# Hi/lo splits of the first dense expert blocks, moved from VectorE to GpSimd

## The chip, the cores and the metric

The kernel runs on one core of a Trainium2 chip. The metric is the device time of one execution in microseconds (us), the median of several runs. The core has a tensor engine (PE in the profile, with its weight loads as PEld), VectorE (DVE), ScalarE (ACT), GpSimd (POOL) and SyncE (SP, which here only issues DMAs). GpSimd also issues the gathers of table rows, as indirect DMAs. Each engine works through its own queue in order.

## The reference

One layer of a decoder, for 1024 prompt positions and 8 x 4 sample positions together (1056 tokens of 1024 features, float32): an RWKV-7 mixer and a pooling mixer with their projections, then a PEER feed-forward, then a gated per-layer embedding and a last norm. The change concerns PEER, cut here to what matters:

```python
q = (xb @ wq).reshape(PEER_BLOCK, PEER_HEADS, 2, PEER_DK_HALF)
s1 = jnp.einsum('thc,nc->thn', q[:, :, 0], sub_keys[0])
s2 = jnp.einsum('thc,nc->thn', q[:, :, 1], sub_keys[1])
v1, i1 = lax.top_k(s1, PEER_TOPK)
v2, i2 = lax.top_k(s2, PEER_TOPK)
...
sc, ci = lax.top_k(cand, PEER_TOPK)
...
expert = e1 * N_KEYS + e2
gate = jax.nn.softmax(sc.astype(jnp.float32), axis=-1)
ue = jnp.take(u_tab, expert, axis=0)
act = jax.nn.gelu(jnp.einsum('thkd,td->thk', ue, xb), approximate=False) * gate
ve = jnp.take(v_tab, expert, axis=0)
return jnp.einsum('thk,thkd->td', act, ve)
```

For each token and each of 8 heads, 16 of 16384 experts are chosen by two top-16 lists over 128 keys each and a top-16 over their sums. Each chosen expert is one row of a table u (a dot product with the token, then gelu times the gate) and one row of a table v (added with that weight).

## The kernel before

The kernel is one program in which a scheduler sets each engine's order: instructions are given in program order, and it places them by that order as priority and by when it takes their inputs to be ready. The order of each queue is fixed when the program is built.

**Stages.** Up to about 1380 us of the profile come the projections, the two mixers, the output projection, and for all tokens the queries and key scores of PEER. Then two ways of computing PEER run side by side:

- Tokens 0 to 671 (GA to GB, ND = 672 columns) are done densely, over all 16384 experts. The experts lie in 128 blocks of 128 (EB = 128). The gates of a token, zero for the experts that it hasn't chosen, were built before and lie in HBM (g_d).
- Tokens 672 to 1055 (384 columns in three tiles of 128) are done by rows: each chosen row of u and v is gathered, and VectorE multiplies and adds (lines 1193 to 1233). For a tile that is 256 gathers. They are issued on GpSimd (line 1202), into 7 row buffers (NROW). The u rows meet line 1210 on VectorE, the v rows lines 1217 and 1219.

**The float32 products in three parts.** A float32 product is made as three products of a faster form: both factors are split into a high part (a rounded copy, made on ScalarE) and a low part (the difference, made with one subtraction), and high x high, high x low and low x high are added up in PSUM. The low parts are what the change moves. Function `esplit` (lines 1065 to 1072) loads a weight block of 128 x 1024 (eraw, 3 buffers, a 512 KB DMA on SP), makes ehi on ScalarE (line 1069, 2 buffers) and elo with the operation that it is given (line 1071, 2 buffers). Function `emm` (lines 1087 to 1093) issues the 48 products of one weight block: 8 blocks of the contracted dimension, three parts each, two halves of 336 columns.

**The dense loop.** For expert block b:

- `ublock(b)` (line 1095) splits the u weights, multiplies them with the tokens (XH, XL) and puts gelu of the result into U[b] (line 1099). For blocks 0 to 7 this was done earlier, by `upre` (line 1101), whose splits are already on GpSimd: `PTT` (line 123) is GpSimd's tensor_tensor, and the profile shows all its instructions under line 124. `TT` is VectorE's.
- `ugate(b)` (line 1144) multiplies with the gates (line 1150, VectorE), copies to the high part wh (line 1152, ScalarE) and subtracts to the low part wl (line 1154). wh and wl have 9 buffers each, in the pool dw, which is opened (line 1140) when the pools of the query stage have been closed (cstack, line 1139). The last users of those pools are the products with the keys on line 747.
- After each eight blocks (VG = 8) `vblock(g, db)` runs for the 8 output blocks db: it splits a block of the v weights, multiplies it with the eight wh and wl, and puts the sum into OT[db] (line 1164 for the first group, line 1162, an addition on VectorE, for the later ones). One group with its 8 output blocks is called a sum, or a round, here.

`dense(0, NB0)` with NB0 = 18 runs blocks 0 to 17 and the sums of groups 0 and 1. It stands in the program between `gtop(0)` and the other two calls of `gtop` (lines 1134 to 1138 and 1182). `gtop` makes the top-16 lists for one tile of the row part (function `top`, line 753): long sequences of max, index search and replacement on VectorE, with some small products on GpSimd (codes, line 793 by way of line 124; one-hot times gate, line 848, whose sum is taken on VectorE, line 850). Only after the third `gtop` are the pools closed whose memory the row buffers take (line 1184), so the gathers start after it. `dense(NB0, EB + 1)` (line 1191) runs the rest of the dense part, and the row part stands behind it in the program and fills in.

At the end come the gated embedding and the last norm, for the dense tokens (`td`) and the tokens of the row part (`tg`).

Of the kernel before, what the change touches and what calls it, by code (L numbers as in the profile page):

```python
# [10 lines left out]
F32 = mybir.dt.float32  # L11
# [5 lines left out]
ALU = mybir.AluOpType  # L17
# [34 lines left out]
VG = 8  # L52
# [9 lines left out]
def body(ctx, tc, io):  # L62
    nc = tc.nc
    mm = nc.tensor.matmul
    TT, STT, TS, ACT = (nc.vector.tensor_tensor, nc.vector.scalar_tensor_tensor, nc.vector.tensor_scalar,
                        nc.scalar.activation)
# [995 lines left out]
    def PD():  # L1062
        return dps.tile([128, 2, 512], F32, name="pd")

    def esplit(src, sub=TT):
        raw = dr.tile([128, KB, 128], F32, name="eraw", bufs=3)
        nc.sync.dma_start(raw, src)
        hi = dr.tile([128, KB, 128], F32R, name="ehi", bufs=2)
        ACT(hi, raw, AF.Copy)  # L1069
        lo = dr.tile([128, KB, 128], F32R, name="elo", bufs=2)  # L1070
        sub(lo, raw, hi.bitcast(F32), op=ALU.subtract)  # L1071
        return hi, lo
# [3 lines left out]
    def otile(db):  # L1076
        if db not in OT:
            OT[db] = (dr if db < KB - 1 else late).tile([128, ND], F32, name=f"OT{db}")
        return OT[db]

    def wt_tile():
        return late.tile([128, ND], F32, name="wt", bufs=NWT)

    def halves(t):
        return t.rearrange("p (a b) -> p a b", a=2)

    def emm(ps, w, xs, parts):
        wh_, wl_ = w
        for k in range(KB):
            xh, xl = xs[k]  # L1090
            for w_, x_, first, last in ((wh_, xh, k == 0, False), (wh_, xl, False, False), (wl_, xh, False, k == KB - 1)):
                for a, (s, n) in enumerate(parts):
                    mm(ps[:, a, :n], w_[:, k, :], x_[:, s:s + n], start=first, stop=last)  # L1093

    def ublock(b, sub=TT):
        ps = PD()
        emm(ps, esplit(io["uT"][b], sub), xs, DP)
        U[b] = otile(b) if b < NPRE else wt_tile()
        ACT(halves(U[b]), ps[:, :, :NH], AF.Gelu)
# [41 lines left out]

    Ws, gqs = {}, {}

    def ugate(b):
        if b % GQ == 0:
            gqs[0] = gqp.tile([128, NTC, GQ, TC], F32, name="gq")
            nc.sync.dma_start(gqs[0], g_d[b // GQ])
        wt_ = U[b]
        w3 = wt_.rearrange("p (c t) -> p c t", t=TC)
        TT(w3, w3, gqs[0][:, :, b % GQ, :], op=ALU.mult)  # L1150
        wh = dw.tile([128, ND], F32R, name="wh", bufs=VG + 1)
        ACT(wh, wt_, AF.Copy)
        wl = dw.tile([128, ND], F32R, name="wl", bufs=VG + 1)
        TT(wl, wt_, wh.bitcast(F32), op=ALU.subtract)
        Ws[b] = (wh, wl)

    def vblock(g, db):
        w = esplit(io["vP"][g, db])
        ps = PD()
        emm(ps, w, [Ws[b] for b in range(g * VG, (g + 1) * VG)], DP)  # L1160
        if g:
            TT(halves(OT[db]), ps[:, :, :NH], halves(OT[db]), op=ALU.add)  # L1162
        else:
            ACT(halves(OT[db]), ps[:, :, :NH], AF.Copy)
        if g == EB // VG // 2:
            ht = wt_tile()
            nc.sync.dma_start(ht, hT_d[:, db, GA:GB])
            TT(OT[db], OT[db], ht, op=ALU.add)

    def dense(b0, b1):  # L1170
        for b in range(b0, b1):
            if b < EB:
                if b not in U:
                    ublock(b)
                ugate(b)
            if b % VG == 0 and b:
                for db in range(KB):
                    vblock(b // VG - 1, db)

    NB0 = 2 * VG + 2  # L1180
    dense(0, NB0)
    for col in range(128, GT, 128):
        gtop(col)
    phases.close()
# [4 lines left out]
    dpt = ctx.enter_context(tc.tile_pool(name="dpt", bufs=2, space=bass.MemoryType.PSUM, reuse_waits="tile"))  # L1189

    dense(NB0, EB + 1)

    for col in range(0, GT, 128):
# [185 lines left out]
def program(arrays, extra=()):  # L1379
    nc = bacc.Bacc("TRN2", target_bir_lowering=False, num_devices=1)  # L1380
    io = {k: nc.dram_tensor(k, v.shape, mybir.dt.from_np(v.dtype), kind="ExternalInput").ap()
          for k, v in arrays.items()}
    for k, s in list(OUTS.items()) + list(extra):
        io[k] = nc.dram_tensor(k, s, F32, kind="ExternalOutput").ap()
    with tile.TileContext(nc, schedule_with_timeline_sim=True) as tc, ExitStack() as ctx:
        body(ctx, tc, io)
    return nc
# [15 lines left out]
```

## Time and profile before

| | us |
|---|---|
| median of 3 runs | 3357.13 |
| lowest and highest run | 3352.67, 3357.15 |
| the profiled execution | 3346.63 |
| its span, first to last instruction | 3344.9 |

| engine, in the profiled execution | busy us | share |
|---|---|---|
| PE | 3163.4 | 95% |
| PEld | 3063.6 | 92% |
| VectorE | 2661.9 | 80% |
| ScalarE | 1187.9 | 36% |
| GpSimd | 1803.7 | 54% |

The profile comes from one execution. It shows busy time by engine, by slices of the span and by groups of like instructions (line, engine, operation, output and inputs by the program's names, count, busy time and mean, then the idle time of the engine ahead of them and what ended it). In views of one tile or line, the three numbers after the count are the shortest, median and longest duration in ns, then the first and last start. A view in order of time has the start, the duration, the engine, the line and the operation; several like instructions in a row are one entry with xN. The chain of waits is followed back from the last instruction: at each step to what released it. The granted clock of the tensor engine is given as a share of its full speed; its mean over the span is 0.980. Matmuls are pipelined, and their ends are modelled.

### The profile page before, as it was taken

What the parts mean: (1) busy time and instruction counts of PE and PEld (TensorE: products, weight loads), DVE (VectorE), ACT (ScalarE), POOL (GpSimd) and SP (SyncE); (2) the same over time, 40 slices, a digit from 0 to 9 for tenths busy, and PEclk for the clock granted to TensorE, in tenths of its full rate; (3) what the DMA queues carried; (4) which work ended last, traced back from release to release, by engine and by line L of the source; (5) the groups of instructions that cost most, each with busy time, mean ns of one, the idle gap of its engine ahead of it and who ended that gap; (6) DMA issues with size and microseconds to landing.
All of it is one profiled execution on the core that took longest, in us unless ns stands there. A gap on an engine that the chain in (4) does not pass through costs nothing.

```text
span 3344.9 us, 57622 instructions
## 1 busy us (share of the span) xinstructions
PE 3163.4 (95%) x21831; PEld 3063.6 (92%) x21831; DVE 2661.9 (80%) x5365; ACT 1187.9 (36%) x1778; POOL 1803.7 (54%) x1434
## 2 busy tenths in 40 slices
PE   8997999998888888999999999999999999999997
PEld 7886989988878777899999999999999999999997
DVE  6777332359999989889888888888889888888966
ACT  6452523345555555431222222122122222222243
POOL 5434333235565456337666666666566666666635
PEclk9998999999999989999999999999999999999998
DMA  5568645667677787639999999999999999999933
GB/s 176 204 218 199 170 134 144 196 193 228 199 198 232 207 290 222 233 128 366 341 339 328 344 349 331 329 340 334 336 337 350 325 335 339 342 328 341 324 110 128
DMA packets 467861, 883.61 MB, mean 264 GB/s; under 512 B 129280, under 2 KB 252416, under 8 KB 463104
## 3 DMA queue, kind: packets, MB, share of 16 engines
q1 hardware_dynamic: 356992, 477.24, 44.3%
q0 software_dynamic: 110592, 402.70, 32.8%
q8 instruction: 171, 2.80, 0.3%
q14 instruction: 106, 0.87, 0.1%
HBM read 759.22 MB, written 120.60 MB: 263 GB/s over the span
## 4 chain that ended last, share of the span: by engine, by line
PE 69%; DVE 16%; DMA 4%; POOL 2%; issue 2%; ACT 1%; SPq 0%; DVEq 0%; ACTq 0%; POOLq 0%
PE pd L1093 57%; DVE ab L882 3%; DVE ab L883 2%; PE ps L663 1%; PE ps L661 1%; PE ps L662 1%; PE ps L526 1%; DMA sraw<-wq 1%; PE ps L521 1%; DVE oh L847 1%; DVE h L718 1%; DVE I L763 1%; DVE s L765 1%; DVE ab L884 1%; DVE I L767 1%
## 5 line engine op out<-in xcount | busy, mean ns | idle before, releaser
L1202 POOL DMA_INDIRECT row<-v,idx x384 | 543.4, 1415 | 314.2 <-DVE po L1219 142.6
L1202 POOL DMA_INDIRECT row<-u,idx x384 | 536.4, 1397 | 284.9 <-DVE row L1210 112.3
L1069 ACT ACTIVATE ehi<-eraw 128x1024 fp32r<-128x1024 f32 x278 | 295.0, 1061 | 1098.3 <-PE pd L1093 955.2
L1093 PE MATMUL pd<-XH,elo 128*128 128x336 f32 x2176 | 516.2, 318 | 6.1 <-DVE elo L1071 3.2
L1093 PE MATMUL pd<-XL,ehi 128*128 128x336 f32 x2176 | 515.4, 318 | 0.0
L1093 PE MATMUL pd<-XH,ehi 128*128 128x336 f32 x2176 | 512.5, 316 | 0.0
L1093 PE MATMUL pd<-wh,ehi 128*128 128x336 f32 (+1 forms) x2112 | 503.0, 317 | 6.2 <-DVE tg L1283 6.2
L1093 PE MATMUL pd<-wl,ehi 128*128 128x336 f32 (+1 forms) x2112 | 503.1, 317 | 0.0
L1093 PE MATMUL pd<-wh,elo 128*128 128x336 f32 (+1 forms) x2112 | 503.0, 317 | 0.0
L1219 DVE SCALAR_TENSOR_TENSOR po<-row,act,po 128x1024 f32<-128x1024 f32 x381 | 488.5, 1282 | 6.5
L1210 DVE SCALAR_TENSOR_TENSOR row<-row,xt 128x1024 f32<-128x1024 f32 x384 | 455.2, 1220 | 5.9 <-DMA row<-u,idx 5.8
L1071 DVE TENSOR_TENSOR elo<-eraw,ehi 128x1024 fp32r<-128x1024 f32 x256 | 318.3, 1243 | 79.8 <-ACT ehi L1069 67.8
L1093 PEld LDWEIGHTS pd<-XH,elo 128*128 128x128 f32 x2176 | 373.8, 189 | 7.8 <-DVE elo L1071 4.3
L1093 PEld LDWEIGHTS pd<-XH,ehi 128*128 128x128 f32 x2176 | 373.0, 189 | 0.3
L1093 PEld LDWEIGHTS pd<-XL,ehi 128*128 128x128 f32 x2176 | 371.2, 189 | 0.2
L1093 PEld LDWEIGHTS pd<-wh,ehi 128*128 128x128 f32 x2112 | 361.5, 188 | 6.9 <-issue 6.7
L1093 PEld LDWEIGHTS pd<-wh,elo 128*128 128x128 f32 x2112 | 362.0, 188 | 0.2
L1093 PEld LDWEIGHTS pd<-wl,ehi 128*128 128x128 f32 x2112 | 361.8, 188 | 0.0
L124 POOL TENSOR_TENSOR ab<-ab,e 128x512 f16<-128x512 f16 x110 | 132.0, 1202 | 160.8 <-DVE ab L883 127.5
L1162 DVE TENSOR_TENSOR OT<-pd,OT 128x672 f32<-128x672 f32 x120 | 102.9, 857 | 139.6 <-PE pd L1093 138.0
L889 ACT ACTIVATE gst<-ps 128x512 f32<-128x512 f32 x168 | 177.1, 1093 | 74.0 <-PE ps L887 72.8
L661 PE MATMUL ps<-hi,whi 128*128 128x256 f32 (+1 forms) x592 | 180.0, 305 | 12.0 <-DMA whi<-wc_d 7.4
(504 smaller groups left out, 5849.7 us busy)
## 6 DMA issues: line engine op xcount, KB each, us to landing
eraw<-uT SPq DMA_DIRECT2D x128, 512.0 KB
eraw<-vP SPq DMA_DIRECT2D x128, 512.0 KB
g_d<-gst SPq DMA_DIRECT2D x21, 2048.0 KB
gq<-g_d SPq DMA_DIRECT2D x32, 1344.0 KB
whi<-wc_d SPq DMA_DIRECT2D x148, 256.0 KB
wlo<-wc_d SPq DMA_DIRECT2D x148, 256.0 KB
wc_d<-shi SPq DMA_DIRECT2D x40, 256.0 KB
wc_d<-slo SPq DMA_DIRECT2D x40, 256.0 KB
```

What stands on the lines that cost most here:

```text
L124: nc.gpsimd.tensor_tensor(out, a, b, op=op)
L661: mm(ps[:, :n], whi[:, kk, :], xhi[:, k, :n], start=k == 0, stop=False)
L882: TT(ab[:, 0:4], iota16[:, None, :, :].to_broadcast([128, 4, EB, 2]), pairs(0, 4), op=ALU.is_equal)
L883: TT(ab[:, 4:6], ab[:, 2:4], pairs(2, 2), op=ALU.mult)
L889: ACT(st[:, :, t2:t2 + 4].rearrange("p e t -> p t e"), v3(ps, 128), AF.Copy, scale=1.0 / GS)
L1069: ACT(hi, raw, AF.Copy)
L1071: sub(lo, raw, hi.bitcast(F32), op=ALU.subtract)
L1093: mm(ps[:, a, :n], w_[:, k, :], x_[:, s:s + n], start=first, stop=last)
L1162: TT(halves(OT[db]), ps[:, :, :NH], halves(OT[db]), op=ALU.add)
L1202: nc.gpsimd.indirect_dma_start(out=r[:m], out_offset=None, in_=io[tab], in_offset=bass.IndirectOffsetOnAxis(ap=idx[:m, hh, k:k + 1], axis=0))
L1210: STT(r[:m], r[:m], 1.0, xt[:m], op0=ALU.mult, op1=ALU.mult, accum_out=pre[:m, k:k + 1])
L1219: STT(po[:m], r[:m], act[:m, k:k + 1], po[:m], op0=ALU.mult, op1=ALU.add)
```

## The change

The functions `ugate`, `vblock` and `dense` take a parameter `sub`, the operation that makes the low parts, and hand it on to `ublock` and `esplit`. Its default is VectorE's `TT`. The first call, `dense(0, NB0)`, now passes `PTT`, GpSimd's. In that call these instructions move from VectorE to GpSimd: elo of the u weights of blocks 8 to 17 (blocks 0 to 7 were made on GpSimd before, in `upre`), elo of the v weights of the sums of groups 0 and 1 (16 blocks), and wl of blocks 0 to 17. Each computes the same difference. The gate product (line 1150), the copies on ScalarE, the additions to OT and all DMAs stay on their engines, and the second call of `dense` is as before.

```diff
-    def ugate(b):
+    def ugate(b, sub=TT):
...
         wl = dw.tile([128, ND], F32R, name="wl", bufs=VG + 1)
-        TT(wl, wt_, wh.bitcast(F32), op=ALU.subtract)
+        sub(wl, wt_, wh.bitcast(F32), op=ALU.subtract)
         Ws[b] = (wh, wl)
 
-    def vblock(g, db):
-        w = esplit(io["vP"][g, db])
+    def vblock(g, db, sub=TT):
+        w = esplit(io["vP"][g, db], sub)
...
-    def dense(b0, b1):
+    def dense(b0, b1, sub=TT):
         for b in range(b0, b1):
             if b < EB:
                 if b not in U:
-                    ublock(b)
-                ugate(b)
+                    ublock(b, sub)
+                ugate(b, sub)
             if b % VG == 0 and b:
                 for db in range(KB):
-                    vblock(b // VG - 1, db)
+                    vblock(b // VG - 1, db, sub)
 
     NB0 = 2 * VG + 2
-    dense(0, NB0)
+    dense(0, NB0, PTT)
     for col in range(128, GT, 128):
         gtop(col)
```

## The prediction

> **What bounds the kernel now.** I read the page first, for where the tensor engine is full.
>
> ```profile
> span 3344.9 us, 57622 instructions
> PE   8997999998888888999999999999999999999997
> PEclk9998999999999989999999999999999999999998
> ```
>
> A slice is 83.6 us. From the seventeenth on (1338 us) PE is at nine tenths or more, to the last slice. The change touches work that starts at about 1386 us, so I then read the chain of work that ended last, in order of time, from there.
>
> ```profile
> 1388.41 3.67 PE pd L1093 x22
> ...
> 1393.19 114.30 PE pd L1093 x742
> 1507.49 1.21 DVE row L1210 x3
> 1508.70 1.15 DVE elo L1071
> 1509.90 543.09 PE pd L1093 x3525
> ...
> 3189.20 41.26 PE pd L1093 x267
> ...
> 3239.28 48.78 PE pd L1093 x312
> ```
>
> The chain is the dense products on line 1093 without a break, but for one piece of VectorE at 1507.5 us. I cut the stretch into slices of 10 us to see how much PE time is lost there at all.
>
> ```profile
> 1380.00:1390.00 10.00, 8.61 (x67) 8.12 (x66) 8.98 (x24) 5.42 (x7) 2.68 (x1) 1.00 1.00 399
> 1500.00:1510.00 10.00, 7.94 (x53) 7.66 (x51) 8.84 (x14) 2.33 (x3) 8.17 (x7) 1.00 1.00 400
> 1510.00:1520.00 10.00, 10.00 (x55) 10.00 (x56) 10.00 (x15) 4.43 (x6) 8.48 (x6) 0.83 0.95 364
> 1520.00:1530.00 10.00, 10.00 (x67) 10.00 (x66) 8.50 (x14) 1.96 (x3) 8.17 (x7) 1.00 0.99 388
> ```
>
> The columns are PE, PEld, DVE, ACT and POOL busy, then the granted clock and the DMA share. A full slice holds 67 products (0.15 us each). The two slices at 1500 us hold 53 and 55, so 26 are missing: 4.0 us, of which 2.06 is PE idle and 1.9 is the clock at 0.83 behind it. At 1380 us 1.4 us are idle and the clock stays at 1.00. So the stretch that the change works on has about 5 us to give back, whatever VectorE is relieved of. The relief itself is off the chain.
>
> **The splits and their prices.** In blocks 0 to 17 and in sums 0 and 1 the low halves go from VectorE to GpSimd: 10 of the u weights (blocks 0 to 7 are there already), 16 of the v weights, 18 of wl. No DMA is moved and SP's queue is unchanged. GpSimd's price for both shapes stands in the trace.
>
> ```profile
> L124 POOL TENSOR_TENSOR elo<-eraw,ehi x22: 2349/2410/3056, 1200.5 to 3320.0; 128x1024 fp32r<-128x1024 f32 x22
> ```
>
> ```profile
> L124 POOL TENSOR_TENSOR wl<-wl,tt x6: 1642/1647/2514, 3247.8 to 3283.4; 128x672 f32<-128x672 f32 x6
> ```
>
> A weight split costs 2.41 us and a wl of 672 columns 1.65 us (this row is another operation on the same shape; the weight row scaled by 672/1024 gives 1.58). GpSimd takes on 26 x 2.41 + 18 x 1.65 = 92.4 us. What stands behind a split on its queue is the top-k's small products (their gl reductions on VectorE wait) and the gathers.
>
> **Step 1, the burst at the first sum.** All eight wl of the first sum are made at once.
>
> ```profile
> 1391.91 1.28 PE L747 MATMUL ps<-keys,q 128*128 128x128 f32 x10
> ...
> 1396.42 0.47 PE L1093 MATMUL pd<-wh,ehi 128*128 128x336 f32 x2
> 1396.73 0.47 PE L1093 MATMUL pd<-wl,ehi 128*128 128x336 f32 x2
> ...
> 1397.34 0.47 PE L1093 MATMUL pd<-wh,ehi 128*128 128x336 f32 x2
> ```
>
> ```profile
> 1393.72 5.34 ACT L1152 ACTIVATE wh<-OT 128x672 fp32r<-128x672 f32 x8
> ```
>
> ```profile
> 1394.51 6.24 DVE L1154 TENSOR_TENSOR wl<-OT,wh 128x672 fp32r<-128x672 f32 x8 [1.10 <-ACT wh L1152]
> ```
>
> The wh cannot start before 1393.2: their buffers (dw) open only when the phase that ends with line 747 is closed. PE begins the sum at 1396.42 and goes one step (0.92 us) per block, so it wants wl number k at 1396.73 + 0.92 k, the last at 1403.2. VectorE makes one in 0.78 us and stays ahead. GpSimd, from 1394.5 at 1.65 us each, ends the last at 1407.7: PE stalls 4.5 us. Then wl of block 8, which stands ahead in program order, ends at 1409.4 and the next weight split at 1411.8, where PE wants it at 1408.9: 2.9 us more. A stall of that size is followed by a lower clock in the row at 1510 us, 1.9 us. Sum 9.3 us; with the block-8 wl behind the weight split and no clock loss it is 4.5 + 1.2 = 5.7. No slack covers this: PE has no other product that is ready. I take 9.3, as the order written in the program gives it. The split of u block 8, which VectorE does late at 1387.2, comes 0.5 us sooner: -0.5.
>
> By "TensorE: Matmul & The Clock Gate" of the Trainium skill (Part 1, What's actually happening) the clock falls to half only after an idle window of about 3.4 us. The trace's drop follows 2.06 us of idle, so by the page step 1 would cost 1.9 us less, and the measurement decides.
>
> **Step 2, the stall at 1507.5 goes.** There the weight split stands on VectorE behind row products that wait for their rows. On GpSimd it doesn't: -4.0 us.
>
> **Step 3, the splits beside the gathers.** The top-k is bound by VectorE, and the gathers start when it ends.
>
> ```profile
> 1492.72 0.41 DVE L850 TENSOR_REDUCE gl<-oh 128x16 f32<-128x256 f32 x1
> ...
> 1493.42 1.50 POOL L1202 DMA_INDIRECT row<-u,idx  x1 [1.71 <-DVE gl L850]
> ```
>
> ```profile
> L1071 DVE TENSOR_TENSOR elo<-eraw,ehi 128x1024 fp32r<-128x1024 f32 x15 | 20.6, 1370 | 0.2 <-ACT ehi L1069 0.2
> ...
> L1154 DVE TENSOR_TENSOR wl<-OT,wh 128x672 fp32r<-128x672 f32 x8 | 6.2, 853 | 1.1 <-ACT wh L1152 1.1
> ...
> L1154 DVE TENSOR_TENSOR wl<-wt,wh 128x672 fp32r<-128x672 f32 x4 | 4.0, 989 | 0.2 <-ACT wh L1152 0.2
> ```
>
> These are VectorE's splits between 1386 and 1493 us: 30.8 us, so the top-k ends up to 31 us sooner, at about 1465, and the gathers with it. The sums and blocks do not move, since PE sets them. One block or one sum is a slot of 7.35 us, the distance between two weight conversions on ACT:
>
> ```profile
> 1447.84 1.06 ACT L1069 ACTIVATE ehi<-eraw 128x1024 fp32r<-128x1024 f32 x1 [5.68 <-PE pd L1093]
> ...
> 1455.19 1.06 ACT L1069 ACTIVATE ehi<-eraw 128x1024 fp32r<-128x1024 f32 x1 [5.68 <-PE pd L1093]
> ```
>
> From 1396.4 on come 8 slots of the first sum, 8 blocks (9 to 16), 8 slots of the second sum and block 17. At 1465 the first sum and about two blocks are over; about 7 blocks and 8 sum slots are left, and in them GpSimd now does splits and gathers. The gathers, in the undisturbed stretch from 1600 to 3100 us, and the waits from 1380 us on:
>
> ```profile
> L1202 POOL DMA_INDIRECT row<-v,idx x343 | 486.2, 1417 | 289.9 <-DVE po L1219 133.6 <-DVE row L1210 96.7 <-issue 48.1
> L1202 POOL DMA_INDIRECT row<-u,idx x336 | 470.1, 1399 | 256.0 <-DVE row L1210 101.0 <-DVE po L1219 95.9 <-issue 48.2
> ```
>
> ```profile
> POOL row L1202 <- issue: 112.4, 368, 0.6
> ```
>
> 679 gathers in 1500 us are 3.33 per slot, each 1.41 us and 0.30 of issue: 5.7 us of GpSimd. A block slot then needs 2.41 + 1.65 + 5.7 = 9.8 us, 2.4 too many; a sum slot 2.41 + 5.7 = 8.1, 0.75 too many. The queue is in order, its order is fixed when the program is built, and PE waits for the split. Upper end: 7 x 2.4 + 8 x 0.75 = 22.8, less the lead of a split (made one slot ahead: 7.35 + 0.6 until it is wanted, less 1.06 + 2.41) of 4.5: 18.3 us. Lower end: 0, if the order holds only the gathers that fit (1.9 and 2.9 per slot). The trace doesn't show which; I take the middle, 9.2. The gathers lost there cost nothing:
>
> ```profile
> L1231 DVE TENSOR_TENSOR row<-pt,row x6: 680/686/692, 2053.5 to 3189.4; 128x512 f32<-128x512 f32 x6
> ```
>
> This is the last step of the row part, at 3189, and by the chain PE has products of line 1093 until 3288.
>
> **Sum.** 9.3 - 0.5 - 4.0 + 9.2 = +14.0 us. The profiled execution took 3346.63 us (the span and 1.7 around it): 3360.6. It lies 10.5 us under the median of the three runs, 3357.13, and I put the difference on the median: 3371 us. What a measurement of this kernel can tell from no change is about 0.2%, 6.7 us.
>
> **Rivals.**
>
> Only the burst costs. The order leaves GpSimd room and step 3 is 0: 9.3 - 0.5 - 4.0 = +4.8, 3362 us, no change that can be told. For it: splits come before gathers in the program, so a split that is ready is queued first. Against: how long a gather is thought to take when the order is made is unknown. Chance 0.27.
>
> Faster. The place is the tail, where PE has this wait:
>
> ```profile
> PE pd L1093 <- DVE tg L1283: 6.2, 2, 5.7
> ```
>
> If rows that end 30 us sooner clear VectorE there, 6.2 us go, with the 4.5 of steps 1 and 2: -10.7, 3346 us. It decides only if the burst costs under 4 us, for which PE would have to find other work, and step 3 nothing. Against: PE has its products until 3288 whenever the rows end. Chance 0.10.
>
> The lock. VectorE's two-input operations and GpSimd's hold each other up:
>
> ```profile
> 3289.04 0.86 DVE L1286 TENSOR_TENSOR OT<-OT,tt 128x672 f32<-128x672 f32 x1 [0.39 <-POOL tt L124]
> 3289.10 3.06 POOL L124 TENSOR_TENSOR elo<-eraw,ehi 128x1024 fp32r<-128x1024 f32 x1
> 3289.81 2.76 DVE L1285 TENSOR_TENSOR tg<-tg,gq 128x384 f32<-128x384 f32 x1
> ```
>
> ```profile
> L1285 DVE TENSOR_TENSOR tg<-tg,gq x8: 558/560/2757, 3289.8 to 3330.4; 128x384 f32<-128x384 f32 x8
> ```
>
> The split took 3.06 instead of 2.41, ending 2.3 us after VectorE's next product began, and that product 2.76 instead of 0.56. So a split costs VectorE, beside row products, up to its own 2.41 where it cost 1.2 when VectorE did it. With 3.33 row products of 1.25 (the mean of these two rows)
>
> ```profile
> L1219 DVE SCALAR_TENSOR_TENSOR po<-row,act,po 128x1024 f32<-128x1024 f32 x381 | 488.5, 1282 | 6.5
> L1210 DVE SCALAR_TENSOR_TENSOR row<-row,xt 128x1024 f32<-128x1024 f32 x384 | 455.2, 1220 | 5.9 <-DMA row<-u,idx 5.8
> ```
>
> and 4.06 us of splits a block slot asks 8.2 us of VectorE as well; rows come free late, the gathers that wait for them hold the next split, and GpSimd's upper end is paid: 9.3 - 0.5 - 4.0 + 18.3 = +23, 3380 us. With 4.2 gathers per slot, as the relieved VectorE could invite, block and sum slots are 3.9 and 2.2 over: 27 + 18 - 4.5 = 40, in all +45, 3402 us. "SBUF — State Buffer" of the Trainium skill (Who interferes with whom) says the same: an exclusive lock that the second to come waits out. Chance 0.20.
>
> **How the numbers follow.** The forecast, step 3 half paid, gets the rest, 0.43. The range reaches from 3354 (between the faster case and the burst alone) to 3392 (inside the lock case); some 0.10 is left out on either side. Faster by over 0.2% is the second rival, 0.10; the same is the first, 0.27; slower is the forecast and the lock, 0.63.
>
> **What would show it.** Right: PE idle of some 7 us between 1396 and 1412 with the wait on POOL's wl and elo of line 124; no wait on DVE elo near 1507; the first gather near 1465; PE waits on POOL's elo in the block slots after it, smaller ones in the sum slots, none behind block 17; the row part still ending near 3190. Wrong: PE full from 1396 to 1580, or the loss in another place, above all in the tail or ahead of 1386 us, which no step touches.

## The result and the profile after

The changed kernel takes 3403.07 us (median of 4 runs, 3401.32 to 3410.3), against 3357.14 for the kernel before (4 runs): a ratio of 1.0144, with a 95% interval of 1.0129 to 1.0159. It is slower by 46 us, over three times the 14 forecast.

The page of the kernel after:

```profile
span 3402.5 us, 57625 instructions
PE   8997999998988888888999999999999999999997
PEclk9998999999999989999999999999999999999998
```

A slice is now 85.1 us. The slices from 1361 to 1616 us (the seventeenth to the nineteenth) are at eight tenths. Behind them the tensor engine is as full as before. To find where the time lies, I cut the stretch by PE's rows in order of time: the first product of v00, of block 9 and of block 18, where the call with GpSimd's splits is over. The kernel before:

```profile
1455.30 0.46 PE L1093 MATMUL pd<-XH,ehi 128*128 128x336 f32 x2
...
1584.69 0.47 PE L1093 MATMUL pd<-XH,ehi 128*128 128x336 f32 x2
```

The kernel after:

```profile
1403.28 0.46 PE L1093 MATMUL pd<-wh,ehi 128*128 128x336 f32 x2
...
1476.54 0.47 PE L1093 MATMUL pd<-XH,ehi 128*128 128x336 f32 x2
...
1639.61 0.47 PE L1093 MATMUL pd<-XH,ehi 128*128 128x336 f32 x2
```

Before, v00 starts at 1396.42, a row that the prediction shows, so the stretch is 188.3 us; after it is 236.3. That is 48.1 more, about the whole difference. (The two profiled spans differ by 57.6; the rest is 6.9 ahead of v00 and 2.7 behind block 18. That v00 starts 7 us later is not the change's doing: the profiled execution of before was a quick one, 10.5 us under the median, and in the three runs below that leave everything ahead of v00 as before it starts at 1407 to 1410.) The first sum takes 73.3 us in place of 58.9, blocks 9 to 16 take 85.6 in place of 63.0, the second sum 68.4 in place of 59.0, and block 17 takes 9.1 in place of 7.4. Before's 63.0 hold the one stall of 4.0 us; the other blocks took 7.4 each. (The expectations of the first two runs below have 48.4 for the growth and 34 for its part behind the first sum; it is 48.1 and 33.7.)

PE's waits between 1380 and 1700 us, after (engine, tile and line, what it waited for; us in all, times, longest):

```profile
PE pd L1093 <- POOL elo L124: 22.4, 11, 6.6
PE pd L1093 <- ACT OT L1164: 7.5, 1, 7.5
PE pd L1093 <- ACT wt L1099: 2.7, 3, 0.9
PE pd L1093 <- POOL wl L124: 1.9, 4, 0.8
```

Before, the same view had 3.4 us in all, 3.2 of it on VectorE's elo. These waits come to 34.5 us, 31 more than before. About 10 of the other 17 are the lower clock behind them: 0.93 and 0.90 in the two stretches of 100 us from 1400 on, where before had 1.00 and 0.98, less some 5 us of low clock that fell into the waits themselves. The rest probably lies in the waits too, which this view counts short, since the ends of products are modelled. In slices of 10 us (PE, PEld, DVE, ACT, POOL busy; clock; DMA share), around the two longest waits:

```profile
1410.00:1420.00 10.00, 3.95 (x21) 2.85 (x19) 10.00 (x34) 0.00 (x0) 8.05 (x5) 0.89 0.01 5
1420.00:1430.00 10.00, 7.36 (x32) 7.36 (x33) 9.52 (x92) 3.77 (x6) 5.06 (x9) 0.60 0.43 132
...
1500.00:1510.00 10.00, 4.77 (x30) 4.21 (x28) 3.62 (x7) 2.27 (x3) 8.14 (x8) 0.82 0.76 259
1510.00:1520.00 10.00, 7.68 (x37) 7.69 (x38) 8.99 (x11) 0.76 (x1) 9.52 (x5) 0.66 0.88 338
```

Where a full slice held 67 products, the second of each pair holds 32 and 37, at 0.60 and 0.66 of the clock.

**The first sum.** The order of time on GpSimd, VectorE, ScalarE and PE, after:

```profile
1400.81 13.36 POOL L124 TENSOR_TENSOR wl<-OT,wh 128x672 fp32r<-128x672 f32 x8 [2.58 <-ACT wh L1152]
1414.14 2.35 POOL L124 TENSOR_TENSOR elo<-eraw,ehi 128x1024 fp32r<-128x1024 f32 x1
1416.45 1.59 POOL L124 TENSOR_TENSOR wl<-wt,wh 128x672 fp32r<-128x672 f32 x1
```

```profile
1412.33 5.88 DVE L793 TENSOR_TENSOR cand<-V 128x64 f32<-128x64 f32 x5
```

```profile
1420.32 0.71 ACT L776 ACTIVATE F<-I 128x128 f32<-128x128 uint32 x2 [11.56 <-DVE I L767]
1420.94 1.04 ACT L1069 ACTIVATE ehi<-eraw 128x1024 fp32r<-128x1024 f32 x1
1421.88 0.71 ACT L1164 ACTIVATE OT<-pd 128x672 f32<-128x672 f32 x1
```

```profile
1422.64 0.93 PE L1093 MATMUL pd<-wh,ehi 128*128 128x336 f32 x2 [7.53 <-ACT OT L1164]
```

GpSimd makes the eight wl in a row, as foreseen, and PE waits for four of them, 0.4 to 0.8 each. The large wait is another one. VectorE's additions that make the top-k's candidates (cand, the sums of the two lists) have two inputs in SBUF. Five of them take 5.88 us, and they end at 1418.2, when GpSimd is through with its row of splits; the longest three take 1.63, 2.39 and 1.63, about what one split takes. The kernel before had them at

```profile
1405.67 0.53 DVE L793 TENSOR_TENSOR cand<-V 128x64 f32<-128x64 f32 x4
1406.32 0.20 DVE L793 TENSOR_TENSOR cand<-V 128x48 f32<-128x48 f32 x1
```

The top-k's index I comes late, ScalarE waits 11.56 us for it at F (the copy of the indices to float, line 776), and behind F in ScalarE's order stands the copy that empties PE's accumulator (OT, line 1164). PE waits 7.53 us for a copy of 0.71.

That this copy stands behind F is itself new. Before, the first output block's copy ran ahead of F:

```profile
1405.26 0.71 ACT L1164 ACTIVATE OT<-pd 128x672 f32<-128x672 f32 x1
1409.58 0.71 ACT L776 ACTIVATE F<-I 128x128 f32<-128x128 uint32 x2 [3.61 <-DVE I L767]
```

So two things come together: F is late, and the order that was fixed with the splits on GpSimd has put the copy behind it. PE's own order adds to it: the elo of 1414.14 was ready at 1416.49, but the first product that uses it stands behind products that wait for the copy, and runs at 1423.93.

**The gathers.** GpSimd's groups of instructions from 1500 to 1640 us (count | busy, mean ns | idle ahead), first before, then after:

```profile
L1202 POOL DMA_INDIRECT row<-u,idx x38 | 55.6, 1464 | 21.4 <-DVE po L1219 7.1 <-issue 7.0 <-DVE row L1210 6.7
L1202 POOL DMA_INDIRECT row<-v,idx x32 | 44.8, 1401 | 18.7 <-DVE po L1219 7.8 <-issue 4.6 <-DVE row L1210 3.3
```

```profile
L1202 POOL DMA_INDIRECT row<-u,idx x32 | 44.5, 1389 | 9.0 <-issue 6.9 <-DVE gl L850 0.7 <-DVE OT L1162 0.6
L124 POOL TENSOR_TENSOR elo<-eraw,ehi 128x1024 fp32r<-128x1024 f32 x14 | 34.5, 2464 | 0.3
L1202 POOL DMA_INDIRECT row<-v,idx x26 | 34.0, 1306 | 6.6 <-issue 5.8 <-DVE OT L1162 0.6
L124 POOL TENSOR_TENSOR wl<-wt,wh 128x672 fp32r<-128x672 f32 x7 | 13.1, 1864 | 0.1
```

After, 126.1 us busy and 16.0 of gaps, mostly issue, fill the 140 us: GpSimd is never free. Those 140 us hold blocks 12 to 17 and the second sum, 14 slots, which took 107 us before, the one stall among them. So GpSimd's work for 140 us was put into slots for 107, 58 gathers among it, 4.1 in a slot.

One loss lies ahead of all gathers. At 1494.71 PE waits 2.68 us for the elo of block 11, which stood on GpSimd behind the top-k's products oh, and they had waited for VectorE; the block takes 11.9 us instead of 7.4.

### The profile page after: what moved, and what is told of

It reads as the page before. It is cut to its first block, busy times and chain, and to the rows that moved or that the text cites. A ratio compares the mean times of both kernels' runs of the same rounds, so it can differ in the third digit from the quotient of the medians.

```text
span 3402.5 us, 57625 instructions
## 1 busy us (share of the span) xinstructions
PE 3188.4 (94%) x21831; PEld 3081.9 (91%) x21831; DVE 2666.2 (78%) x5321; ACT 1183.2 (35%) x1776; POOL 1898.4 (56%) x1478
## 4 chain that ended last, share of the span: by engine, by line
PE 65%; DVE 16%; DMA 6%; POOL 3%; issue 2%; ACT 1%; SPq 1%; DVEq 0%; ACTq 0%; POOLq 0%
PE pd L1093 53%; DVE ab L882 3%; DVE ab L883 2%; PE ps L663 2%; PE ps L661 2%; PE ps L662 1%; PE ps L526 1%; DMA sraw<-wq 1%; DVE oh L847 1%; PE ps L521 1%; DMA wlo<-wc_d 1%; DVE h L718 1%; POOL elo L124 1%; DVE I L763 1%; DVE cand L793 1%
## 5 line engine op out<-in xcount | busy, mean ns | idle before, releaser
L1202 POOL DMA_INDIRECT row<-u,idx x384 | 543.7, 1416 | 279.7 <-DVE row L1210 104.4
L1219 DVE SCALAR_TENSOR_TENSOR po<-row,act,po 128x1024 f32<-128x1024 f32 x381 | 499.8, 1312 | 8.7 <-DMA row<-v,idx 2.2
L1210 DVE SCALAR_TENSOR_TENSOR row<-row,xt 128x1024 f32<-128x1024 f32 x384 | 464.3, 1243 | 14.9 <-DMA row<-u,idx 14.8
L1071 DVE TENSOR_TENSOR elo<-eraw,ehi 128x1024 fp32r<-128x1024 f32 x230 | 284.8, 1238 | 73.4 <-ACT ehi L1069 67.5
```

The source lines that it names most:

```text
L1202: nc.gpsimd.indirect_dma_start(out=r[:m], out_offset=None, in_=io[tab], in_offset=bass.IndirectOffsetOnAxis(ap=idx[:m, hh, k:k + 1], axis=0))
L1210: STT(r[:m], r[:m], 1.0, xt[:m], op0=ALU.mult, op1=ALU.mult, accum_out=pre[:m, k:k + 1])
L1219: STT(po[:m], r[:m], act[:m, k:k + 1], po[:m], op0=ALU.mult, op1=ALU.add)
```

## The experiments

In each run the stages were cut as above. Their excess over before (58.9, 63.0, 59.0 and, for block 17, 7.4 us) stands in this table beside the time measured. A run without any stall in blocks 9 to 16 has -4 there:

| run | first sum | blocks 9 to 16 | second sum | block 17 | sum, us | ratio to before, 95% interval |
|---|---|---|---|---|---|---|
| changed kernel | +14.4 | +22.5 | +9.4 | +1.7 | +48.1 | 1.0144, 1.0129 to 1.0159 |
| first round alone | +14.6 | +2.6 | -0.1 | 0 | +17 | 1.0042, 1.0026 to 1.0059 |
| second round alone | 0 | +16.4 | +12.1 | +0.3 | +29 | 1.0089, 1.0068 to 1.0109 |
| gathers behind the splits | +14.7 | -1.2 | -0.1 | 0 | +13 | 1.0144, 1.0124 to 1.0164 |
| gathers behind u16 | +14.6 | -1.2 | +14.1 | +0.4 | +28 | 1.0082, 1.0057 to 1.0107 |
| twins | +28.4 | +2.4 | -0.1 | 0 | +31 | 1.0236, 1.0215 to 1.0257 |
| writes only | +7.9 | +42.4 | +10.8 | 0 | +61 | 1.0175, 1.0158 to 1.0192 |
| late wl | 0 | +3.7 | +1.6 | 0 | +5 | 1.0011, 0.9999 to 1.0024 |
| late elo | +0.1 | +9.7 | +3.1 | +1.1 | +14 | 1.0042, 1.0029 to 1.0055 |
| early elo | +1.3 | -0.3 | -0.1 | 0 | +1 | 1.0000, 0.9985 to 1.0014 |
| early wl | +10.9 | -3.9 | -0.1 | 0 | +7 | 1.0029, 1.0017 to 1.0042 |
| elo up to u14 | +1.2 | +12.5 | -0.1 | 0 | +14 | 1.0040, 1.0024 to 1.0057 |
| elo, then gathers | +1.2 | +2.2 | -0.1 | 0 | +3 | 0.9995, 0.9986 to 1.0004 |

One thousandth is 3.4 us. Except in two runs, which lose time at the end as well, the excess by stage agrees with the time measured within 6 us.

Two theories stood against each other. The queue: GpSimd takes its instructions in order, splits and gathers do not fit into a slot together, and PE waits for the split. The lock: VectorE's two-input operations and GpSimd's splits hold each other up, and the time is lost through VectorE.

**First round alone, second round alone.** The change cut in two, at block 8 (the second run has > for <=).

```diff
-                    ublock(b, sub)
-                ugate(b, sub)
+                    ublock(b, sub if b <= VG else TT)
+                ugate(b, sub if b <= VG else TT)
...
-                    vblock(b // VG - 1, db, sub)
+                    vblock(b // VG - 1, db, sub if b <= VG else TT)
```

> GpSimd makes the splits only as far as the first round of sums (the weights of blocks 0 to 8, u8, and v00 to v07); blocks 9 to 17 and the second round split on VectorE again. In the changed kernel the stretch from v00 to the end of the second round grew by 48.4 us over before: 14.4 of them in the first sum, 34 in the blocks and sums behind it. Both theories (the queue: GpSimd's instructions in order do not fit into the slots where splits and gathers meet; the lock: VectorE's two-input operations and GpSimd's splits hold each other up) put the burst's cost into the first sum, so both expect about 14 us above before, 3371 us, and 3366 to 3376 is agreement. A third view, that the program's new order of instructions and not the place of the splits costs the time, would have no reason to divide in this way. In the stretch behind the first sum both expect the stall of 4.0 us at VectorE's late elo, or more of it, because the top-k ends late.

> The complement: VectorE splits as far as the first round of sums, GpSimd from block 9 to the end of the second round, where the gathers of the first row tile are. Both theories expect the cost behind the first sum to stay, about 34 us above before, 3391 us, and none in the first sum (58.9 us there). If the burst's delay of the top-k was what pushed gathers and splits together, less would be left: with the first gather where it was before (1493 us) the overlap begins at the same block, so I expect 28 to 38 us. The sum of this and the other part should be the whole 46 within 6 us; if it is far from that, the two parts feed each other.

3376.12 and 3390.41 us, against 3362.39 for before in the same job: 14 and 28, which make 42 of the 46 to 48. The parts add up, and each part of the loss stays where its splits are. That does not refute the third view for the first sum: in this run and in every other that keeps the row of eight wl on GpSimd and takes it into use, ScalarE's order has F ahead of the first copy OT, and in before and in the runs that lose 1.3 us or less there it has the copy ahead. The burst alone does not bring the overlap with it. The second round's 28 us, the low edge of what was expected, are lost although nothing ahead of them was delayed.

**Gathers behind the splits.** The changed kernel with the gathers of the first row tile issued on GpSimd behind its last split.

```diff
+    last_split = lastp[0]
...
+            with tc.issue_after(last_split) if col == 0 else nullcontext():
```

> The changed kernel, with one thing moved: the gathers of the first row tile are issued on GpSimd behind its last split, so no gather lies between two splits. The queue theory: the waits of TensorE for elo (22.4 us on the matmul side, 26.4 on the weight side) go, the blocks u9 to u16 take about 63 us and the second sum about 59, and only the burst's 14 us are left: 3371 us, or less by the 4.0 us stall that VectorE's late elo gave before: 3367; the row work starts some 150 us later, which costs at the end only if it had less slack than that. The lock theory expects part of the cost to stay where VectorE's two-input operations lie beside the splits: but the products of the first row tile are also later, so it expects the overlap's cost to fall too, to 5 to 15 us above the burst's 14: 3376 to 3386. A time near 3403 would refute the queue.

3409.99 us, so the time is as bad as ever, but the stages say why: blocks and second sum are back at 61.8 and 58.9 us. Without gathers between them the same splits on the same engine cost next to nothing there: the wait at block 11 is left, 2.68 us as in the changed kernel, and takes back most of the 4.0 us of before's stall, which is gone. The time went to the end instead. The slice from 3100 to 3300 us:

```profile
3100.00:3300.00 200.00, 172.16 (x1092) 169.28 (x1091) 183.03 (x206) 51.82 (x62) 136.10 (x95) 0.94 0.88 308
```

PE was full there before (200.00); now it waits for row work that started 100 us later (first gather at 1599.68 in place of 1499.33) and has VectorE at 183. So the row work did not have that much slack, and the total alone would have refuted a theory that the stages uphold.

**Gathers behind u16.** The same, with the gathers behind the splits of block 16 only (the edit against the run above).

```diff
-    last_split = lastp[0]
+    last_split = lastp[1]
...
+            if b == 2 * VG:
+                lastp[1] = lastp[0]
```

> The changed kernel with the gathers of the first row tile issued on GpSimd behind the splits of the block u16, so that the blocks u9 to u16 see no gather between their splits and the second sum still does. The queue theory: the blocks take about 63 us (85.6 in the changed kernel), the second sum still loses 5 to 12, the first its 14; the row work starts some 50 us later than in the changed kernel. With every gather behind the last split it started about 110 us later and the kernel lost about 34 us at its end, so that some 75 us of delay are free, and this delay costs nothing: 3357 + 14 + 9 = 3380, and 3374 to 3388 is agreement. If the end loses in proportion to the delay, without slack, it is 3390 to 3400.

3388.05 against 3363.72. The blocks are as in the run above, and the second sum, where gathers and elo meet, loses 14 us, a little more than the 5 to 12 expected. The gathers started at 1528.60, 29 us later than in the changed kernel, and PE is full to 3300 again: a delay of that size costs nothing.

**Twins.** VectorE makes each split, and GpSimd makes it once more into a tile that nobody reads.

```diff
+    def TWIN(out, a, b, op):
...
+        PTT(t, a, b, op=op)
+        return TT(out, a, b, op=op)
...
-    dense(0, NB0, PTT)
+    dense(0, NB0, TWIN)
```

> VectorE makes every split, as before, and TensorE takes its results; GpSimd makes the same subtractions a second time, at the same places of its order, into a tile that nobody reads. So GpSimd's queue and its accesses to memory are those of the changed kernel, but TensorE waits for none of its splits. The queue theory: TensorE loses almost nothing; the gathers come as late as in the changed kernel, with slack, so the time is within 8 us of before: 3357 to 3365. The lock theory: VectorE now has the splits and is also held up by GpSimd's twins, so TensorE waits for VectorE instead: at least half of the 46 us stays, 3380 or more. If the first sum keeps its 14 us here, they come through VectorE and the top-k (cand to ScalarE's F to OT and ehi), not through the wait for wl or elo.

3441.17 us, 79 above before: outside the queue's range and inside the lock's, but the run did not test what it was made for. All gathers came behind the twins (the first at 1637.47; probably since the twin's tile lies in memory that the row work takes over), so nothing met in the blocks, and the end lost as in the run with the gathers behind the splits. What it does show is the first sum: 28 us lost although PE takes none of GpSimd's results. VectorE's own wl are held beside the twins, 14.10 us for seven of them where eight took 6.24 before; the candidates, which come behind, are not (0.63 us for five). From 1390 to 1640 us PE waits 12.8 us for VectorE's elo and wl and 14.3 us, in two waits, for ScalarE's ehi; the first of these ehi waits in its turn 3.95 us for a twin that has still to read the buffer. So part of this loss comes through VectorE alone, but not all of it: a twin's place on GpSimd still reaches PE through ehi.

**Writes only.** GpSimd's splits replaced by a subtraction of one column and three fills, which read nothing; the low parts of these blocks are left out of the result.

```diff
+        PTT(out[one], a[one], b[one], op=op)
...
+        nc.gpsimd.memset(o, 0.0)
+        nc.gpsimd.memset(o, 0.0)
+        nc.gpsimd.memset(o[:, :n // 2], 0.0)
```

> GpSimd's splits of the changed kernel are replaced by writes of about the same length: a subtraction of one column, which keeps the wait for ScalarE's high half, and three fills of the low half's tile with zeros (128x1024, 128x1024 and 128x512 for elo, the same shares for wl), which read nothing. The low halves of these blocks are so left out of the result. GpSimd's queue is as full as in the changed kernel, and TensorE waits for it in the same way; only the reading of SBUF is gone. The queue theory: the blocks and sums behind the first sum still lose about 30 us, or more, since gathers can now lie between the parts of one split, and the whole stays at 3390 or above. The lock theory: VectorE's two-input operations run free; the first sum returns to about 60 us, its candidates to 0.5 us each, the gathers and splits to a shorter round, and at most a third of the 46 us is left: 3372 or less. A first sum that comes back while the later part stays would give the burst to the lock and the overlap to the queue: about 3387 to 3392.

3422.61 us against 3361.95, 61 above: in the queue's range, and over the 3387 to 3392 of the mixed case. By stage it divides the two. In the first sum the lock's part goes: the candidates take

```profile
1417.58 0.63 DVE L793 TENSOR_TENSOR cand<-V 128x64 f32<-128x64 f32 x5
```

instead of 5.88 us, PE's wait for OT falls from 7.5 to 1.5, and of 14.4 us 7.9 are left. ScalarE's order is the changed kernel's here, with the copy behind F; no run has held candidates with the copy ahead of F, except for a single one of 1.63 us in the runs with the early elo, so how much of the 7.5 us the new order is answerable for is open. "SBUF — State Buffer" of the Trainium skill (Who interferes with whom) states that a VectorE instruction with two SBUF inputs contends with a GpSimd instruction that reads SBUF, and not with one that only writes it; the candidates' 5.88 beside splits and 0.63 beside fills agree. In the blocks the time is lost as before and more. The waits of PE from 1500 to 1660 us, and VectorE's group of gate products from 1500 to 1640 in this run, then the same group in the changed kernel:

```profile
PE pd L1093 <- POOL elo L1188: 41.0, 9, 10.2
```

```profile
L1150 DVE TENSOR_TENSOR wt<-wt,gq 128x672 f32<-128x672 f32 x6 | 5.1, 857 | 17.9 <-ACT wt L1099 12.9 <-POOL wl L1187 5.0
```

```profile
L1150 DVE TENSOR_TENSOR wt<-wt,gq 128x672 f32<-128x672 f32 x6 | 14.8, 2471 | 11.5 <-ACT wt L1099 11.5
```

VectorE's products run at 0.86 instead of 2.47 us, so the lock is gone, and PE waits for GpSimd's elo all the more. (More, since one split is four instructions here, 3.1 us instead of 2.46, with gathers in between.) The overlap's cost does not need the lock; with a queue that is so much fuller the run does not say how much of the 34 us the lock adds.

**Late wl, late elo.** Of the second round's splits only wl, or only elo, on GpSimd (shown for wl; for elo TT and the condition change places, and the sums have it too).

```diff
-                    ublock(b, sub)
-                ugate(b, sub)
+                    ublock(b, TT)
+                ugate(b, sub if b > VG else TT)
```

> Of the second part's splits (28 us above before by themselves) only those of the weights of blocks 9 to 17 are on GpSimd (9 of 1.6 us, 15 us); every elo and the whole first round are on VectorE. GpSimd had 27 us free of 100 between 1500 and 1600 us in the kernel before, 2.0 us in a slot of 7.35. The queue theory: 1.6 us in a slot fits, so it costs little: 0 to 6 us. The lock theory counts the time for which both read: 15 us of 56 us of splits, so about a quarter of the 28: 5 to 10 us.

> The other half of the second part: each elo of blocks 9 to 17 and of v10 to v17 on GpSimd (17 of 2.4 us, 41 us), all wl on VectorE. The queue theory: 2.4 us in each slot is over the 2.0 us that were free, and each elo stands behind one to four gathers of about 1.7 us, so most of the 28 us stays: 15 to 28 us. The lock theory, by time: three quarters of 28, 18 to 23. The two differ here in where it is lost: by the queue TensorE waits for GpSimd's elo and VectorE is idle; by the lock VectorE's products and sums are longer. If this and the run with wl alone together give far less than 28, there is a threshold in the slot, which only the queue has.

3365.42 and 3375.1 against 3361.95. The first is 3.5 above, which the interval does not tell from nothing: the queue's range, under the lock's. The second is 13 above, a little under both ranges. Together 17, where both at once cost 28: as by a threshold in the slot, one kind of split finds some room between the gathers, and both do not. Most of the 13 is a single wait: at 1517.42 PE waits 7.24 us for one elo behind the first gathers, and that block takes 10 us longer. The same wait stands in the changed kernel (6.65 us) and in the second round alone (6.91).

**Early elo, early wl.** The same division of the first round.

> Only the elo of the blocks up to u8 and of v00 to v07 are on GpSimd, no wl, and nothing behind v07. The burst of eight wl in a row on GpSimd, beside which VectorE's candidates took 5.88 us instead of 0.53 each, is gone. If that burst is what costs the 14 us in the first sum (through the late top-k and what stands behind it on ScalarE), the first sum is within 3 us of before's 58.9, and the time is between 4 below (VectorE is relieved of nine splits, and its late elo of 1507 us comes in time) and 3 above before: 3353 to 3362 against 3357. If single elo beside the top-k hold VectorE up as well, the first sum loses 4 to 10 us: 3361 to 3367.

> The complement of the run with the early elo alone: only the weight splits of blocks 0 to 8 are on GpSimd, nine of 1.6 us that come in one row at the first sum, and every elo and everything behind is on VectorE. If that row is what costs the first sum its 14 us, by TensorE's wait for each wl and by VectorE's candidates that it holds up (5.88 us for five instead of 0.53 each, then ScalarE's F, then the add into OT), all of it is here: 3367 to 3373 against 3357, with a first sum of about 70 us. If the elo behind the row are needed for it, less than half remains: 3364 or below.

3360.72 against 3361.95, and 3372.41 against 3363.72. The elo of the first round cost nothing; the row of wl costs 9 to 11 us by itself, against the 10 to 16 that were expected. In that run too the candidates are held, and the copy stands behind F:

```profile
1425.64 4.27 DVE L793 TENSOR_TENSOR cand<-V 128x64 f32<-128x64 f32 x5
```

The remaining 2 or 3 of the first sum's 14.4 come only with both; how was not taken apart.

**Elo up to u14, and elo before the gathers.** The candidate from these runs (its edit is below), and the same with the elo up to u16 and the gathers issued behind the last of them, as in the run with the gathers behind the splits.

```diff
-                    ublock(b, sub)
-                ugate(b, sub)
+                    ublock(b, sub if b <= VG + 6 else TT)
+                ugate(b, TT)
...
-                    vblock(b // VG - 1, db, sub)
+                    vblock(b // VG - 1, db, sub if b <= VG else TT)
```

> The candidate: only elo on GpSimd, no wl, in the first round (u8, v00 to v07, as in the run with the early elo alone) and for the blocks up to u14, which lie mostly ahead of the gathers; all else on VectorE. In the run with the early elo alone TensorE still waited 2.5 us once for VectorE's elo, at about 1500 us, and 2.1 us in all for GpSimd's elo. If the late elo is the one of u13 or u14, its wait goes, and two or three elo meet gathers: by the queue theory that costs up to 3 us each, as in the run with the late elo. So both theories leave it between 4 below and 4 above before: 3353 to 3361 against 3357; I do not expect the measurement to tell it from no change, and a time clearly below before would be the first version that beats it.

3376.71 against 3363.72, 13 us slower and outside what was expected. One elo costs most of it. GpSimd in order of time (the idle time ahead and its cause in brackets), then PE:

```profile
1503.05 1.16 POOL L1202 DMA_INDIRECT row<-u,idx  x1 [1.72 <-DVE gl L850]
...
1510.73 1.91 POOL L1202 DMA_INDIRECT row<-u,idx  x1 [0.30 <-issue]
1512.66 2.36 POOL L124 TENSOR_TENSOR elo<-eraw,ehi 128x1024 fp32r<-128x1024 f32 x1
```

```profile
1515.07 0.93 PE L1093 MATMUL pd<-XH,elo 128*128 128x336 f32 x2 [7.32 <-POOL elo L124]
```

The elo stands behind seven gathers (as many as there are row buffers), and these had waited for the top-k's last step (gl). The changed kernel has the same place, with 6.65 us of waiting at 1512.32.

> In the run with the elo up to u14 on GpSimd, one elo alone cost most: it stood on GpSimd behind seven gathers that had waited for the top-k's last index, and TensorE waited 7.3 us for it and then ran at a lower clock. Here the elo of u8, of v00 to v07 and of u9 to u16 are on GpSimd, every wl and the second round on VectorE, and the gathers of the first row tile are issued behind the last of these elo, some 30 to 40 us later than in before. If it is the place in the queue behind the gathers that costs, and not that splits and top-k or splits and row work run at the same time, the blocks u9 to u16 take 62 to 64 us and nothing else is lost: 3353 to 3361 against 3357, at best 4 below by the stall of before that is gone. If the run at the same time costs anyway, it stays at 3367 or above.

3362.45 against 3361.41, a ratio of 0.9995 (0.9986 to 1.0004). With the same elo and more of them on GpSimd, but ahead of the gathers, the blocks lose 2.2 us in place of 12.5, and no wait stands between 1500 and 1660 us. What is left is one wait ahead of that:

```profile
PE pd L1097 <- ACT wt L1103: 3.1, 1, 3.1
```

So VectorE can be relieved of these splits at no cost that the measurement shows, and nothing is gained by it either: the stall of before is gone, and this wait has taken its place. None of the versions beats the kernel before.

## Why the prediction was wrong

The direction and the place were right: slower, in the stretch that the steps named, with PE full again behind block 17. The size failed, 46 us against 14.

**Step 3, the splits beside the gathers, is the step that failed.** It forecast 9.2 us, the middle between a lower end (the order holds only the gathers that fit) and an upper end of 18.3; measured are 22.5, 9.4 and 1.7, together 33.7, and 28 for the second round by itself. Two terms were too small. First, the middle: the order left no gather out for the splits' sake, so the upper end was due. Second, that end: it took 3.33 gathers a slot, the mean from 1600 to 3100 us; in the slots of the change there are 4.1. Before, it was 70 in the 140 us, 3.7 per 7.35 us, and a view of that stretch would have said so. With 4.1 the step's own arithmetic (2.41 + 1.65 + 4.1 x 1.71 in a block slot, 2.41 + 4.1 x 1.71 in a sum slot) gives 3.7 and 2.1 us too many; blocks 12 to 16 had 4.0 (57.3 us, 11.5 each, less 7.5), the sum slots 1.2. That the first pair agrees is in part luck, for half of what those blocks lost is one wait. The step left this latency out: one elo behind seven gathers costs 7 us of waiting and the clock's drop, 10 us in all, whatever the throughput. It left out block 11 too, where 4.5 us went without a gather, behind the top-k's small products, which the prediction had standing behind a split only, not ahead of one.

**"The top-k ends up to 31 us sooner" failed too.** The first gather after:

```profile
1499.33 1.50 POOL L1202 DMA_INDIRECT row<-u,idx  x1 [0.75 <-DVE gl L850]
```

That is 96.1 us after v00, as against 97.0 before (1493.42 less 1396.42). The top-k is no chain on VectorE alone. VectorE's waits from 1396 to 1500 us, after:

```profile
DVE gl L850 <- POOL oh L124: 6.9, 5, 3.0
DVE wt L1150 <- ACT wt L1099: 6.3, 1, 6.3
DVE V L762 <- DMA scq<-sc_d: 3.9, 3, 2.0
```

Before, the first and third were 1.9 and 1.2, and there was no wait on wt. It hands its steps to GpSimd (oh) and ScalarE, and both were now later. Even with the early elo alone, which costs nothing and takes about 12 us of splits off VectorE, the first gather came 90.2 us after v00 (1497.99 less 1407.75), 7 us sooner. With all of the splits away and only writes on GpSimd it came 81.0 us after v00 (1490.42 less 1409.44), 16 us sooner, not 31.

**Step 1, the burst,** was 9.3 less 0.5 and measured 14.4: right in place, half right in mechanism. PE's stall on wl was put at 4.5; the waits on it come to 1.9, and v00's products took about 3.7 us longer than before by their rows, so that this term was near. The 2.9 behind block 8's wl did not arise, since the order has the elo ahead of it. In its place stands the wait of 7.5 through the candidates, F and OT, of which the run with writes only removes 6.0, and the clock behind it. The prediction took ScalarE's order as unchanged; it was not. That VectorE's two-input operations are held was a rival, but the prediction looked for it beside the row products only, not beside the top-k.

**Step 2** held: VectorE's elo is gone from PE's waits. Its 4 us can't be seen in the total; in the run with the gathers behind the splits the blocks are 1.2 us shorter than before, the 4 us less what block 11 lost.

**The rivals.** The lock's second figure, +45 with 4.2 gathers a slot, is what was measured. Half of it was the right cause, 4.1 gathers a slot, on the queue alone; that the number came out is luck, since it counts seven blocks and eight sums at the full rate and puts 9.3 into the first sum. Its first half, that VectorE holds the gathers up, is not what sets the overlap's cost, by the run with writes only; its share in the rest can be bounded from there, as an estimate: 58 gathers at 1.22 us instead of 1.35, and 21 splits that are 0.05 to 0.2 longer beside VectorE, are some 10 of GpSimd's 140 us. "Only the burst" and "Faster" are refuted. The row part ended later, not near 3190:

```profile
L1231 DVE TENSOR_TENSOR row<-pt,row x6: 681/682/692, 2087.7 to 3223.8; 128x512 f32<-128x512 f32 x6
```

It still ends ahead of the products, as the prediction had it, so the gathers lost cost nothing here; with 100 us of delay they do.

## What to carry to other kernels

Work moved to an idle engine is paid by the place it gets in that engine's order: look at what stands ahead of it there in the slots in question (count it there, not as a mean over the kernel), how long it can wait, and who waits behind. GpSimd's idle share of 27% (before, 1500 to 1600 us) was no room, since the order left no gather out for the splits; and when the total stays bad after a repair, cut the span by stage before dropping the theory. A relief of an engine off the chain is worth nothing until its next reader is shown to move, and a move to GpSimd can take back on VectorE what it gives, as it did here with VectorE's operations on two inputs (five candidates 5.88 instead of 0.73 us). And a moved instruction changes the fixed order of engines that it never ran on, as with ScalarE's copy behind F: compare the orders of before and after on each of them.

## What the hardware showed

A gather's instruction on GpSimd takes between 0.93 and 2.0 us: the row of the u gathers in the changed kernel has the shortest, the median and the longest.

```profile
L1202 POOL DMA_INDIRECT row<-u,idx x384: 932/1597/1997, 1499.3 to 3169.3; - x192
```

Three of the first, at 1501 to 1504 us with VectorE waiting, take 0.94 each, and the one at 1506.49, beside a row product that starts at 1506.34, takes 1.88. That VectorE's products lengthen it is what these suggest; no run took it apart. The slice of 10 us in which a stall of 7.53 us ends has a clock of 0.60, that of 6.65 us has 0.66, and the slice right behind before's stall of 2.06 has 0.83. In the clock's own record each of these drops is to one half: for 10.24 us at the two long stalls, for 3.41 us behind the short one.
